# Seven load slots instead of nine for the quads of four feed-forwards, four more scratch blocks, and an earlier read-back of the memory's chunks

## Chip, cores and metric

The kernel runs on one core of one Trainium2 chip. The metric is the device time of one execution, in microseconds (us); less is better. Engines are named as the profile names them: PE does the matrix products (PEld loads its weights), ACT and DVE the elementwise work, POOL little here, and SP mostly issues DMAs.

## What is computed

A two-layer "first block" and then a one-layer "second block" act on 512 tokens of width 1024, in float32. Cut to what matters:

```
def swiglu(h, w_gate, w_up, w_down):
    return (silu(h @ w_gate) * (h @ w_up)) @ w_down          # D_FF = 2816

for l in range(2):                                            # first block
    x = x + 0.5 * swiglu(rmsnorm(x, g_ffn1[l]), ...ffn1[l])
    u = rmsnorm(x, g_mix[l])                                  # mixer: Fourier, dilated and
    ...                                                       # differential attention, gates
    x = x + merged @ w_out[l]
    x = x + 0.5 * swiglu(rmsnorm(x, g_ffn2[l]), ...ffn2[l])
x = rmsnorm(x, g_final)

proj = rmsnorm(x) @ w_in_2                                    # second block ("mixer 2")
attn_o = window_attention(rope(q), rope(k), v, sink)
dn_o   = gated_deltanet(conv(qkv), gate, alpha, beta)         # chunks of 64, 2 directions, 4 heads
x = x + rmsnorm(concat(attn_o, dn_o) @ w_out_2)
x = x + rmsnorm(cross_attention(rmsnorm(x), rmsnorm(mem), w_cq_2, w_ckv_2, w_co_2))
x = x + rmsnorm(swiglu(rmsnorm(x), ...ffn_2))
```

## The kernel before

Every float32 product is done as three products of rounded parts: a weight tile is split into a high part `whi` (by ACT) and the rest `wlo` (by DVE), an activation likewise, and PE adds hi·hi, hi·lo and lo·hi. All weights stream through SBUF once: a 512 KB slab lands in a tile of the pool `raw` (4 KB in each of 128 partitions; five slots), is split into `whi` and `wlo` tiles of 512 columns (pools of five each), and its slot is free again after the last split has read it. Activations and everything else of 512 columns lie in blocks `g` of one pool of NB = 59. Tasks that run beside each other share a count `self.free` of these blocks: `acq(n)` waits until n are free, `rel(n)` gives them back, so NB steers which tasks of a stage may start.

A planner (`drive`) writes the program: tasks are generators with a priority, and the planner's own clock decides which one emits its next instructions. The order on each engine's queue is fixed by the time the kernel is built; on the chip an engine that waits holds everything behind it on its queue. SP's queue issues the weight loads and many small transfers to and from scratch memory in DRAM (`kn_d`, `cs_d`, `nt_d`, `qk_d`, `xinv_d`), in that one order.

**The feed-forwards** (`ffn_task`, four times) begin with a wide start and two pairs of plain slabs (gate and up of columns 256 to 511 and 512 to 767: four raw tiles a pair), and then run eight *quads* n = 0 to 7. A quad takes two feature chunks by a scheme with seven instead of eight products for a two-by-two block product. `fast_load` loads a quad's four weight tiles: two to `raw` (gate, up) and two to the pool `b` (gate, up; four slots); `fast_split(…, 1)` takes a third raw slot for a difference, called q7 here. Nine slots, five raw and four `b`, hold this before. `left(n, i)` puts the splits of product i on the list, `right(n, i)` its matmuls (12 of 256 columns), and `down` puts products of the down projection between them: from quad 2 on, each quad but the last holds two down slabs of 512 KB (four feature chunks each, 24 matmuls of 512 columns); the first six chunks are taken earlier by slabs of 512 KB plus 256 KB (`down(0, 6, …)`). The list runs three items ahead with loads and splits.

**Mixer 2** (`mixer2_task`, from about 2398 us) projects `w_in_2`, runs a convolution, rotary attention in a window and the delta rule (eight chains with triangular inverses through `xinv_d`). Its budget is `self.free = NB - 16 - 9 - 5 - self.mem`. The keys and values of the memory (`memory_proj`, slabs of `w_ckv_2`) run beside it at low priority; that task first reads eight chunks back from DRAM (`mem_d`, on POOL's queue; ten blocks, `self.mem = 10`). `self.rooms` counts the feed-forwards that have reached their last four down slabs. `xinv_d` is set to zero by one DMA of 4128 KB on ACT's queue early in the fourth feed-forward. The list below shows the functions; every instruction of the trace is recorded at line L119, so groups are told apart by tile names.

Of the kernel before, what the change touches and what calls it, by code (L numbers as in the profile page):

```python
# [41 lines left out]
    _o += _w  # L42
MK_COLS = _o
OH_COLS = 1024 + 256 + 64
NB = 59

LK = 4

# [87 lines left out]
class Net:  # L136
    def __init__(self, ctx, tc, ins, dump=None):
        self.ctx, self.tc, self.nc, self.i = ctx, tc, Engines(self, tc.nc), ins
        self.n = 0
        self.dump = dump or {}  # L140
        mk = lambda name, **kw: ctx.enter_context(tc.tile_pool(name=name, **kw))
        self.const = mk("const", bufs=1)
        self.raw = mk("raw", bufs=5)
        self.whi = mk("whi", bufs=5)
        self.wlo = mk("wlo", bufs=5)
        self.pg = mk("pg", bufs=NB)
        self.pt = mk("pt", bufs=2)
        self.psum = mk("psum", bufs=8, space=bass.MemoryType.PSUM)
        self.dram = mk("dram", bufs=1, space=bass.MemoryType.DRAM)

        self.t = 0.0
        self.curp = 9
        self.tasks = []
        self.clk = {"vector": 0.0, "scalar": 0.0, "gpsimd": 0.0}
        self.done = {}
        self.banks = []
        self.ahead = self.gap = False
        self.lock = None
        self.mem, self.kv, self.kvs = 0, [0] * 4, {}
        self.free = NB  # L160
        self.normed = True
        self.rooms = 0
        self.pend = []
# [644 lines left out]
    def ffn_task(self, wg, wu, wd, pre, row, after):  # L808
# [69 lines left out]
        for n in range(nq):  # L878
# [3 lines left out]
                left(n - 1, 4)  # L882
            left(n, 6)
            left(n, 5)
            if n + 1 < nq:
                load(n + 1)
            if n:
                left(n - 1, 3)
            left(n, 7)
            if n == 0:  # L890
                down(0, 6, (4, 6))
            elif n > 1:
                f = 6 + 4 * (n // 2 - 1)
                if n + 1 < nq:
# [737 lines left out]
    def mixer2_task(self, after):  # L1632
        nc, i = self.nc, self.i
        w = i["w_in_2"][0]
        us = self.us
        self.mem = 10
        self.spawn(self.memory_proj(), 7)
        self.free = NB - 16 - 9 - 5 - self.mem
        st = {"cv": {}, "str": False, "k": [False] * 4, "q": [False] * 4, "v": [False] * 4, "nt": [0, 0], "solved": [False] * 2,
              "gate": set(), "win": 0, "B": 0, "dn": 0, "chain": 0}  # L1640
# [641 lines left out]

    def memory_proj(self):
        nc, i = self.nc, self.i
        mp = [(self.g(F32R, [P, 2, 256]), self.g(F32R, [P, 2, 256])) for _ in range(KC // 2)]
        for c in range(KC // 2):
            for k in range(2):
# [267 lines left out]
def build(ctx, tc, ins, out, dump=None, stop=None):  # L2555
# [32 lines left out]
    def between(l):  # L2588
        showx(f"xb{l}")
        if l == 0:  # L2590
            ffn(2, 0, G_FFN1[1], middle)
        else:
            c1.close()
            n.phase(c2, "second")
            ffn(2, 1, G_FINAL, second)
            n.spawn(n.setup_second(), 1)

    def middle():
        showx("xc0")
# [37 lines left out]
```

## Time and profile before

| | us |
|---|---|
| Median of 3 runs | 3406.07 |
| Lowest and highest of them | 3394.13, 3406.7 |
| The profiled execution, its time | 3396.84 |
| Its span | 3395.1 |
| PE busy in it | 3295.8 (97%) |
| DVE busy | 2325.5 (68%) |
| ACT busy | 1562.3 (46%) |

The span is the time between the first and the last instruction of the profiled execution; its time is 1.7 us longer. The stages follow one another: feed-forward 1 to about 375 us, mixer to 850, feed-forwards 2 and 3 to 1190 and 1550, mixer to 2040, feed-forward 4 to 2398, mixer 2 to 2880, cross-attention to 2980, and the last feed-forward. Since PE is busy 97% of the span, the reader looks for the few stretches where it isn't, and for what ended its idle time there.

### The profile page before, as it was taken

What the parts mean: (1) busy time and instruction counts of PE and PEld (TensorE: products, weight loads), DVE (VectorE), ACT (ScalarE), POOL (GpSimd) and SP (SyncE); (2) the same over time, 40 slices, a digit from 0 to 9 for tenths busy, and PEclk for the clock granted to TensorE, in tenths of its full rate; (3) what the DMA queues carried; (4) which work ended last, traced back from release to release, by engine and by line L of the source; (5) the groups of instructions that cost most, each with busy time, mean ns of one, the idle gap of its engine ahead of it and who ended that gap; (6) DMA issues with size and microseconds to landing.
All of it is one profiled execution on the core that took longest, in us unless ns stands there. A gap on an engine that the chain in (4) does not pass through costs nothing.

```text
span 3395.1 us, 50388 instructions
## 1 busy us (share of the span) xinstructions
PE 3295.8 (97%) x19063; PEld 2895.3 (85%) x19063; DVE 2325.5 (68%) x4423; ACT 1562.3 (46%) x3049; POOL 45.2 (1%) x121
## 2 busy tenths in 40 slices
PE   8999999999999999999999999999979888999998
PEld 6899888898889988998888988899868777888887
DVE  6787677656677777776766476777788775764344
ACT  4454545443445454545455444454453344553232
POOL 1000000000000000000000000000000000000000
PEclk9999999999999999999999999999989899999999
DMA  4533433435333333333323368333347522223232
GB/s 134 152 116 94 119 91 93 135 97 181 105 109 110 102 118 100 111 95 118 92 90 118 91 197 159 111 112 94 118 155 203 175 89 91 81 81 100 94 103 70
DMA packets 370948, 391.02 MB, mean 115 GB/s; under 512 B 30801, under 2 KB 325309, under 8 KB 370704
## 3 DMA queue, kind: packets, MB, share of 16 engines
q1 hardware_dynamic: 329248, 332.45, 32.6%
q10 hardware_dynamic: 38464, 47.68, 5.0%
q0 software_dynamic: 2992, 7.67, 0.7%
q8 instruction: 149, 2.44, 0.3%
q14 instruction: 95, 0.78, 0.1%
HBM read 343.56 MB, written 39.98 MB: 113 GB/s over the span
## 4 chain that ended last, share of the span: by engine, by line
PE 89%; DVE 7%; DMA 2%; ACT 1%; issue 1%; SPq 0%; ACTq 0%; DVEq 0%; POOL 0%; POOLq 0%
PE ps L119 89%; DVE g L119 5%; ACT g L119 1%; DVE wlo L119 1%; DMA b<-in_w_ffn_up 0%; DVE sm L119 0%; DMA g<-xinv_d 0%; DMA g<-in_x 0%; DVE b L119 0%; DMA g<-cs_d 0%; ACT whi L119 0%; DVE tmp L119 0%; DMA g<-in_g_ffn 0%; DVE xs L119 0%; SPq L119 0%
## 5 line engine op out<-in xcount | busy, mean ns | idle before, releaser
L119 PE MATMUL ps<-g,whi 128*128 128x512 f32 (+1 forms) x9312 | 2401.4, 348 | 16.0 <-ACT g L119 13.7
L119 PEld LDWEIGHTS ps<-g,whi 128*128 128x128 f32 x9312 | 1620.0, 190 | 234.4 <-ACT g L119 18.4
L119 PE MATMUL ps<-g,wlo 128*128 128x512 f32 (+1 forms) x4656 | 1611.5, 346 | 1.1 <-DVE wlo L119 1.1
L119 ACT ACTIVATE whi<-raw 128x512 fp32r<-128x512 f32 (+1 forms) x1084 | 670.4, 622 | 875.3 <-PE ps L119 776.9
L119 DVE TENSOR_TENSOR wlo<-raw,whi 128x512 fp32r<-128x512 f32 (+1 forms) x1084 | 726.6, 678 | 392.7 <-ACT whi L119 377.7
L119 PEld LDWEIGHTS ps<-g,wlo 128*128 128x128 f32 x4656 | 884.2, 190 | 111.5 <-DVE wlo L119 2.8
L119 DVE TENSOR_TENSOR g<-g,g 128x512 f32<-128x512 f32 (+4 forms) x668 | 401.7, 622 | 74.6 <-ACT g L119 64.8
L119 ACT ACTIVATE g<-g 128x256 fp32r<-128x256 f32 (+4 forms) x560 | 310.7, 571 | 211.8 <-DVE g L119 193.5
L119 DVE TENSOR_TENSOR g<-ps,g 128x512 f32<-128x512 f32 (+3 forms) x350 | 204.2, 598 | 187.5 <-PE ps L119 94.3
L119 PE MATMUL ps<-g,g 128*128 128x128 f32 (+5 forms) x1638 | 264.9, 309 | 14.5 <-DVE g L119 6.3
L119 PE MATMUL ps<-whi,g 128*128 128x256 f32 (+1 forms) x1184 | 255.9, 310 | 0.0
L119 PEld LDWEIGHTS ps<-g,g 128*128 128x128 f32 (+3 forms) x1638 | 223.8, 193 | 35.6 <-DVE g L119 7.2
L119 ACT ACTIVATE whi<-b 128x512 fp32r<-128x512 f32 x192 | 121.2, 632 | 220.5 <-PE ps L119 211.5
L119 DVE SCALAR_TENSOR_TENSOR g<-ps,g 128x512 f32<-128x512 f32 x210 | 149.0, 711 | 98.5 <-PE ps L119 97.8
L119 PEld LDWEIGHTS ps<-whi,g 128*128 128x128 f32 x1184 | 196.6, 192 | 11.3
L119 PE MATMUL ps<-wlo,g 128*128 128x256 f32 (+1 forms) x592 | 183.6, 310 | 3.5 <-DVE wlo L119 3.5
L119 DVE TENSOR_TENSOR wlo<-b,whi 128x512 fp32r<-128x512 f32 x192 | 131.7, 688 | 58.2 <-ACT whi L119 57.9
L119 ACT COPY g<-ps 128x512 f32<-128x512 f32 (+5 forms) x250 | 114.2, 476 | 115.4 <-PE ps L119 103.7
L119 ACT ACTIVATE g<-ps 128x256 fp32r<-128x256 f32 (+6 forms) x239 | 100.3, 433 | 134.2 <-PE ps L119 118.1
L119 DVE TENSOR_TENSOR g<-g,ps 128x512 f32<-128x512 f32 (+1 forms) x171 | 111.4, 655 | 42.1 <-PE ps L119 38.0
L119 PEld LDWEIGHTS ps<-wlo,g 128*128 128x128 f32 x592 | 113.6, 192 | 9.5 <-DVE wlo L119 3.7
L119 ACT ACTIVATE g<-g,sm 128x512 f32<-128x512 f32 (+3 forms) x160 | 89.3, 579 | 37.0 <-DVE sm L119 36.0
(203 smaller groups left out, 1589.8 us busy)
## 6 DMA issues: line engine op xcount, KB each, us to landing
raw<-in_w_ffn_down SPq DMA_DIRECT2D x80, 512.0 KB, 3.4
raw<-in_w_in SPq DMA_DIRECT2D x80, 512.0 KB, 3.9
raw<-in_w_ffn_gate SPq DMA_DIRECT2D x55, 512.0 KB, 3.8
raw<-in_w_ffn_up SPq DMA_DIRECT2D x55, 512.0 KB, 4.0
raw<-in_w_gate SPq DMA_DIRECT2D x48, 512.0 KB, 3.7
raw<-in_w_gate_up SPq DMA_DIRECT2D x44, 512.0 KB, 3.6
b<-in_w_ffn_gate SPq DMA_DIRECT2D x32, 512.0 KB, 3.8
b<-in_w_ffn_up SPq DMA_DIRECT2D x32, 512.0 KB, 3.9
```

The lines of the kernel that those rows point to most:

```text
L119: r = f(*a, **k)
```

## The change

The raw pool has three slots instead of five, which gives 8 KB in each partition; the block pool takes them (63 instead of 59). In a quad the loads of quad n + 1 come on the list after its seventh product instead of after the fifth, and the two early down slabs of chunks 4 to 7 are spread over quads 0 and 1 instead of both standing in quad 0. `memory_proj` is spawned with the fourth feed-forward and waits for `rooms == 4`, so its eight read-backs stand at that feed-forward's end instead of in mixer 2, and `self.mem = 10` is set there.

```diff
-NB = 59
+NB = 63
...
-        self.raw = mk("raw", bufs=5)
+        self.raw = mk("raw", bufs=3)
...
             left(n, 6)
             left(n, 5)
-            if n + 1 < nq:
-                load(n + 1)
             if n:
                 left(n - 1, 3)
             left(n, 7)
-            if n == 0:
-                down(0, 6, (4, 6))
+            if n + 1 < nq:
+                load(n + 1)
+            if n < 2:
+                down(0, 6, (4 + 2 * n,))
...
         us = self.us
-        self.mem = 10
-        self.spawn(self.memory_proj(), 7)
         self.free = NB - 16 - 9 - 5 - self.mem
...
     def memory_proj(self):
         nc, i = self.nc, self.i
+        yield lambda: self.rooms == 4
+        self.mem = 10
...
             ffn(2, 1, G_FINAL, second)
             n.spawn(n.setup_second(), 1)
+            n.spawn(n.memory_proj(), 7)
```

On SP's queue, in a steady quad of the first feed-forward (the numbers behind a tile's name run in the order in which the planner wrote the tiles; `in_w_ffn1_gate` and `_up` are the quad's loads, `_down` the down slabs), it stood so before:

```order
L119 DMA b382_1756<-in_w_ffn1_gate 128x4x256
L119 DMA raw395_1854<-in_w_ffn1_down 128x4x256
L119 DMA raw400_1864<-in_w_ffn1_down 128x4x256
L119 DMA b384_1760<-in_w_ffn1_up 128x4x256
L119 DMA raw438_2095<-in_w_ffn1_gate 128x4x256
L119 DMA raw440_2099<-in_w_ffn1_up 128x4x256
```

and so after:

```order
L119 DMA b448_2164<-in_w_ffn1_gate 128x4x256
L119 DMA raw447_2162<-in_w_ffn1_gate 128x4x256
L119 DMA raw449_2166<-in_w_ffn1_up 128x4x256
L119 DMA b450_2168<-in_w_ffn1_up 128x4x256
L119 DMA raw452_2195<-in_w_ffn1_down 128x4x256
L119 DMA raw461_2244<-in_w_ffn1_down 128x4x256
```

All four loads of the next quad now stand ahead of this quad's two down slabs, and the second down slab was written later (2244 behind 2195, where the two were 10 apart).

On ACT's queue, early in the fourth feed-forward, right behind the zeroing of `xinv_d` (`raw4329` and `raw4330` are the two gate tiles of the slab pair that follows it, `raw4339` and `raw4340` the up tiles, `b43…` tiles of the pool `b` with sums of activations), it stood so before:

```order
L119 ACTIVATE whi4331_21370<-raw4329_21366 128x512
L119 ACTIVATE whi4333_21374<-raw4330_21368 128x512
L119 ACTIVATE g4355_21491<-b4351_21486 128x512
L119 ACTIVATE g4357_21496<-b4353_21488 128x512
L119 ACTIVATE g4359_21501<-b4351_21486 128x512
L119 ACTIVATE whi4335_21378<-raw4329_21366 128x512
L119 ACTIVATE g4361_21506<-b4353_21488 128x512
L119 ACTIVATE whi4337_21382<-raw4330_21368 128x512
```

and so after:

```order
L119 ACTIVATE whi4331_21370<-raw4329_21366 128x512
L119 ACTIVATE g4355_21491<-b4351_21486 128x512
L119 ACTIVATE g4357_21496<-b4353_21488 128x512
L119 ACTIVATE whi4333_21374<-raw4330_21368 128x512
L119 ACTIVATE g4359_21501<-b4351_21486 128x512
L119 ACTIVATE whi4335_21378<-raw4329_21366 128x512
L119 ACTIVATE g4361_21506<-b4353_21488 128x512
L119 ACTIVATE whi4337_21382<-raw4330_21368 128x512
```

Two sums moved ahead of the first split of `raw4330`; that split still stands ahead of the second split of `raw4329`.

On PE, in mixer 2, behind the last `w_in_2` product of the first heads (`ident` rows are transposes; a row with a single `g` spreads per-row factors over a block; `whi51…` with 256 columns are the memory's keys), it stood so before:

```order
L119 MATMUL ps5083_25460<-ident_102,g5031_25193 128x128 x4
L119 MATMUL ps5092_25488<-ident_102,g5032_25205 128x128 x4
L119 MATMUL ps5096_25505<-ident_102,g5054_25328 128x128 x4
L119 MATMUL ps5102_25527<-g5097_25510 128x128 x4
L119 MATMUL ps5106_25545<-ident_102,g5067_25413 128x128 x4
L119 MATMUL ps5108_25552<-g5107_25550 128x128 x4
L119 MATMUL ps5111_25563<-ident_102,g5084_25465 128x128 x4
L119 MATMUL ps5113_25571<-g5112_25568 128x128 x4
L119 MATMUL ps5127_25604<-g5071_25428,whi5118_25587 128x256
```

and so after:

```order
L119 MATMUL ps5095_25521<-ident_102,g5032_25205 128x128 x4
L119 MATMUL ps5099_25534<-ident_102,g5054_25328 128x128 x4
L119 MATMUL ps5102_25543<-g4935_24703,whi5077_25440 128x512
L119 MATMUL ps5102_25543<-g4936_24704,whi5077_25440 128x512
L119 MATMUL ps5102_25543<-g4935_24703,wlo5078_25441 128x512
...
L119 MATMUL ps5104_25560<-g5100_25539 128x128 x4
L119 MATMUL ps5122_25622<-g4935_24703,whi5114_25606 128x512
```

Where eight short groups stood in a row, a `w_in_2` product of 24 matmuls of 512 columns now stands between two of them, and another follows. The slabs of `w_ckv_2` come later in the order than before, behind the other projections.

## Rows read from the trace of the kernel before

**Rows 1.** The page: busy time by engine (part 1), ended chain by engine (part 4).

```profile
PE 3295.8 (97%) x19063; PEld 2895.3 (85%) x19063; DVE 2325.5 (68%) x4423; ACT 1562.3 (46%) x3049; POOL 45.2 (1%) x121
...
PE 89%; DVE 7%; DMA 2%; ACT 1%; issue 1%; SPq 0%; ACTq 0%; DVEq 0%; POOL 0%; POOLq 0%
```

**Rows 2.** Busy times by stretch: length, PE, PEld, DVE, ACT, POOL, clock, DMA.

```profile
850.00:1190.00 340.00, 340.00 (x2102) 307.13 (x2101) 248.66 (x376) 162.93 (x281) 2.19 (x4) 1.00 0.36 105
...
2490.00:2520.00 30.00, 15.69 (x83) 13.68 (x81) 27.74 (x74) 12.30 (x43) 0.00 (x0) 0.73 0.34 113
2520.00:2600.00 80.00, 80.00 (x498) 71.82 (x497) 70.55 (x190) 42.94 (x116) 3.14 (x7) 1.00 0.80 235
2600.00:2660.00 60.00, 56.52 (x348) 49.31 (x347) 44.03 (x81) 20.00 (x40) 0.54 (x1) 0.97 0.61 179
2660.00:2830.00 170.00, 137.68 (x988) 124.23 (x987) 126.11 (x375) 66.41 (x184) 0.00 (x0) 0.92 0.34 104
```

**Rows 3.** PE's waits, 2490 to 2520: total us, times, longest us.

```profile
PE ps L119 <- ACT g L119: 10.8, 3, 7.4
PE ps L119 <- DVE g L119: 3.6, 1, 3.6
```

**Rows 4.** PE's waits, 2660 to 2675.

```profile
PE ps L119 <- DMA g<-qk_d: 4.6, 1, 4.6
PE ps L119 <- DMA g<-xinv_d: 4.6, 2, 3.6
```

**Rows 5.** PE's waits, 170 to 178 (quads 0 and 1 of the first feed-forward).

```profile
PE ps L119 <- ACT g L119: 1.6, 1, 1.6
PE ps L119 <- DVE wlo L119: 0.5, 1, 0.5
```

**Rows 6.** SP's DMA issues in a steady quad: start us, duration us, what.

```profile
1114.59 0.37 SPq L119 DMA_DIRECT2D b<-in_w_ffn_gate  x1
1117.25 3.31 SPq L119 DMA_DIRECT2D raw<-in_w_ffn_down  x2
1123.07 0.37 SPq L119 DMA_DIRECT2D b<-in_w_ffn_up  x1
1129.72 0.37 SPq L119 DMA_DIRECT2D raw<-in_w_ffn_gate  x1
1131.65 0.37 SPq L119 DMA_DIRECT2D raw<-in_w_ffn_up  x1
```

**Rows 7.** DVE, the same quad, in order of time.

```profile
1125.41 0.69 DVE L119 TENSOR_TENSOR wlo<-raw,whi 128x512 fp32r<-128x512 f32 x1
1126.13 1.23 DVE L119 TENSOR_TENSOR raw<-raw,raw 128x1024 f32<-128x1024 f32 x1
```

**Rows 8.** PE, the same quad; the 128x512 rows are a down product.

```profile
1131.62 0.63 PE L119 MATMUL ps<-g,whi 128*128 128x512 f32 x2
...
1137.09 0.62 PE L119 MATMUL ps<-g,whi 128*128 128x512 f32 x2
```

**Rows 9.** DMA issues of the whole run: xcount, KB each, median us to landing.

```profile
raw<-in_w_ffn_down SPq DMA_DIRECT2D x80, 512.0 KB, 3.4
...
xinv_d<-g ACTq DMA_DIRECT2D x1, 4128.0 KB, 42.4
raw<-in_w_ffn_down SPq DMA_DIRECT2D x16, 256.0 KB, 2.6
```

**Rows 10.** Landing times of all down loads (in_w_ffn_down), us min/median/max.

```profile
DMA to landing us min/median/max: 2.6/3.4/8.7
```

**Rows 11.** DMA queues and issues, 2083 to 2126 (q10 is ACT's queue, q1 SP's).

```profile
q10 hardware_dynamic: 8208, 4.23, 79.0%
q1 hardware_dynamic: 3589, 3.56, 35.9%
...
raw<-in_w_ffn_up SPq DMA_DIRECT2D x3, 512.0 KB, 14.3
```

**Rows 12.** Landings of the two raw loads issued between 2094.4 and 2096.3.

```profile
DMA to landing us min/median/max: 16.5/17.7/18.9
```

**Rows 13.** Landing of the raw load issued at 2114.9.

```profile
DMA to landing us min/median/max: 9.8/9.8/9.8
```

**Rows 14.** PE there; the four raw tiles of two slabs are first used here.

```profile
2105.92 0.62 PE L119 MATMUL ps<-g,whi 128*128 128x512 f32 x2
...
2108.64 0.62 PE L119 MATMUL ps<-g,whi 128*128 128x512 f32 x2
...
2111.36 0.62 PE L119 MATMUL ps<-g,whi 128*128 128x512 f32 x2
...
2114.08 0.62 PE L119 MATMUL ps<-g,whi 128*128 128x512 f32 x2
```

**Rows 15.** ACT at the start of the fourth feed-forward.

```profile
2104.59 0.63 ACT L119 ACTIVATE whi<-raw 128x512 fp32r<-128x512 f32 x1 [2.91 <-PE ps L119]
...
2105.65 1.14 ACT L119 ACTIVATE whi<-raw 128x512 fp32r<-128x512 f32 x2
...
2111.06 0.63 ACT L119 ACTIVATE whi<-raw 128x512 fp32r<-128x512 f32 x1 [3.75 <-DMA raw<-in_w_ffn_up]
...
2114.25 0.61 ACT L119 ACTIVATE whi<-raw 128x512 fp32r<-128x512 f32 x1
```

## The prediction

> **What bounds the kernel now.** I read the page first, then the busy times by stretch, then PE's waits in the stretches where PE is not full, then SP's issues and the landing times. The page says that PE is busy 3295.8 of 3395.1 us and that PE's own work is 89% of the chain that ended last [rows 1]. In a feed-forward stretch there is nothing to win: PE is busy 340.00 of 340 us [rows 2]. What there is lies in mixer 2. There PE idles 30 - 15.69 = 14.3 us from 2490 to 2520, nothing from 2520 to 2600, 3.5 us from 2600 to 2660 and 170 - 137.68 = 32.3 us from 2660 to 2830 [rows 2], 50.1 us in all. The first idle stretch waits for results of ACT and DVE, 10.8 and 3.6 us [rows 3], and DVE is busy 27.74 of those 30 us [rows 2]: a chain of small vector work (convolution, norms) with only transposes between on PE. The last one begins with waits for transfers of the delta rule, 4.6 us for `qk_d` and 4.6 for `xinv_d` [rows 4]. TensorE's granted clock is 1.00 of full speed where PE is full and 0.73 and 0.92 in the two idle stretches [rows 2].
>
> So the change takes slots from stages that are full and gives blocks to the one stage that isn't. The working below asks what fewer slots cost there and what four blocks are worth here.
>
> **Steady quads (n = 2 to 7), three raw slots.** Call S the start of a quad's first down product, 1131.62 in the trace; its 24 matmuls end 5.47 us later, at 1137.09, where the second begins [rows 8]. Before, the two down slabs are issued at about 1117.2 and 1120.2 (two issues that take 3.31 us together [rows 6]), 11 us and more ahead of S. After, the three slots are held by gate, up and q7, and the first down slab gets q7's slot of the quad when its last split ends: 1125.41 + 0.69 = 1126.10, that is S - 5.5 [rows 7]. It lands a median 3.4 us later [rows 9], at S - 2.1; ACT's split takes 0.63 [rows 15] and DVE's 0.69 [rows 7], so it is ready at S - 0.8. The second down slab needs the first one's slot, free when both halves are split, about S; it lands at S + 3.4, is ready at S + 4.75, and is wanted at S + 5.47. Margins of 0.8 and 0.7 us, on a path that had 10: at the median nothing, but the slowest landing of the run was 8.7 us [rows 10] and would cost 4 to 5. There are 24 such pairs. I take **+2 us** (a slow landing every tenth slab at half a microsecond); bounds 0 and 15 (0.6 us for each pair). The next quad's gate and up loads, issued at 1129.72 and 1131.65 before and ahead of the down slabs now [rows 6], gain time. What is queued behind the waiting down slab on SP is the next quad's loads, whose slots come free later anyway.
>
> **Quads 0 and 1.** Each now has one slab pair of 512 and 256 KB. The second waits for the first one's slot, issued about S, lands in 2.6 us [rows 9], and has its high part at S + 3.3, its low part at S + 4.0. PE wants them after 12 matmuls of 5.47/24 us, at S + 2.7 and S + 3.2. Short by 0.8 to 0.9 us, eight times: **+7 us**; bounds 0 (the first slab's early halves done sooner) and 16. In the first feed-forward PE waits 1.6 and 0.5 us at this place now [rows 5], behind quad loads that stood behind the down slabs on SP; they now stand ahead: **-2 us**, at best that, at worst 0.
>
> **The start of the fourth feed-forward.** Under the zeroing of `xinv_d` (42.4 us [rows 9], 79.0% of the engines' time from 2083 to 2126 [rows 11]) raw loads land very late: two issued at 2094.5 and 2095.8 after 16.5 and 18.9 us [rows 12], one issued at 2114.9 after 9.8 [rows 13]. Before, four tiles of the next two slabs had landed or were on their way ahead of it, and PE started them at 2105.92, 2108.64, 2111.36 and 2114.08 [rows 14] without a stall, though ACT already waited 3.75 us for one of these transfers [rows 15]. With three slots each load is issued two tiles later. The second tile (2108.64) takes the issue of 2094.5 and lands about 2111.0: 3 us late. The third takes that of 2095.8 and lands at 2114.7: another 1. The fourth needs the slot of `raw4329`, whose second split stands on ACT behind the first split of the late second tile; it is issued near 2114.9, and by the row of that time lands at 2124.7, is split at 2125.3, and is wanted at 2114.08: 11 us in all, the earlier delays included. By the undisturbed 3.7 us it would be 2118.6, 5 us in all. I take the row of the same instant: **+11 us**, bounds 5 and 15.
>
> The Trainium skill says in "DMA: Bandwidth & Descriptors", section "Queues, rings and completion order", that each of the 16 DMA engines goes round the queues that have work, a packet from each. By that a load beside one other queue would get about half the engines, 3.4 us would become 7, and this term would be 0, as an estimate from that page; the 16.5 and 18.9 us of the trace speak against it, and the sum goes by the trace.
>
> **Mixers 1 and the last two stages.** PE is full in the mixers, the SP order of their slabs is the same, and no transfer of a raw tile stands among PE's waits there, so I take three slots to be enough: **0**, bounds -1 and +4. The read-back of the memory's chunks moves eight POOL transfers of 256 KB into the end of the fourth feed-forward, where POOL has no other work and SP's down slabs share the DMA engines: 0, bounds 0 and 3.
>
> **Mixer 2.** With four more blocks the planner puts `w_in_2` products between the transposes where PE stood idle, and the memory's slabs later. Total PE and DVE work is unchanged. From 2490 to 2600 DVE is busy 27.74 + 70.55 = 98.3 of 110 us [rows 2], so the stretch can't shrink by more than 11.7; from 2600 to 2660 the 3.5 us can go. In the last stretch DVE is busy 126.11 of 170 us, so PE's 32.3 us are the bound. All four head pairs now come to the deltas together, which gives more chains beside each other, but less projection work is left to put between. I take 11.7 + 3.5 + a third of 32.3 (10), **-25 us**. Bounds: -50 (every idle stretch), and +15 for the case below.
>
> **The rivals.** (a) *The delta stretch is filled too*: four pairs of chains beside each other cover each other's transfers and PE's clock stays up. For it: the waits there are latency, not work. It gives 50 instead of 25: 3396.84 + 18 - 50 = 3365. (b) *The slots bind in the quads*, the slower side. Place: the two down slabs of a quad, with 0.7 us of margin each. If transfers land 1 us later than the median, because all of a quad's loads now stand together ahead of them on SP, each of 24 pairs costs 1 to 1.3 us, and the early quads 1 us more: 30 + 15 + 11 - 2 - 25 gives 3396.84 + 29 = 3426. It decides from a landing of 4.2 us; the median of 3.4 speaks against it. The Trainium skill's rule in "DMA: Bandwidth & Descriptors", section "Rules for kernel authors", to issue a DMA early and wait for it late, is on this rival's side; the trace has no quad with so late an issue. (c) *The fill is only moved*: products taken for 2490 to 2520 are missing after 2660, the delta chains last as long as before and PE idles 14 us more there. Then mixer 2 gives 0 and the sum is 3396.84 + 18 = 3415. It decides if the stretch of the deltas doesn't get shorter than its 170 us. (d) *The change doesn't do what it says*, the blocks go unused: the order on PE speaks against it, since the products already stand elsewhere.
>
> **How the numbers follow.** The sum is +2 +7 -2 +11 +0 -25 = -7 us against the profiled execution, 3396.84: 3390. That execution lies 9.2 us under the median of the runs shown, 3406.07; against the median it is 3399. The runs lie in two groups some 12 us apart, and I can't tell in which the median after falls, so I predict the middle, **3394 us**. Its own range, with the terms' bounds, is 3375 to 3415. Chances: this forecast 0.46, (a) 0.22, (b) 0.13, (c) 0.16, (d) 0.03. The range for 8 in 10 reaches from (a) to the near part of (b): 3364 to 3422. A measurement of this kernel can tell about 0.5%, 17 us, from no change. Faster than 3389 are all of (a) and a third of the forecast, 0.38; slower than 3423 are most of (b) and a third of (c), 0.17; within, 0.45.
>
> **What would show it.** Right: PE stays full in the steady quads, with short waits for `wlo` or `whi` twice in each feed-forward's quads 0 and 1; one wait of some 11 us in two or three pieces near 2105 to 2125, behind raw loads under the zeroing; PE almost full from 2490 to 2520, and the deltas' end some 10 to 15 us nearer to the start of mixer 2 than before even after that. Wrong: waits for raw loads in every quad (b); the idle time reappearing in the delta stretch, with no shorter mixer 2 (c); a delta stretch with PE above 95% and the clock at 1.00 (a). The largest guess is the third of the 32.3 us; the next is the landing under the zeroing.

## The result: 20 us slower, where a few microseconds less were forecast

The changed kernel takes 3419.41 us (median of 5 runs, 3417.32 to 3424.64), the kernel before 3399.27 us (median of 5, 3394.13 to 3406.7). The ratio is 1.0058, with a 95% interval of 1.0039 to 1.0076. The forecast was 3394 us; the time lies inside the range (3364 to 3422) but on the other side of no change. The spans of the two profiled executions are 3395.1 and 3415.5 us, so the traces hold the same 20 us.

The page of the changed kernel, busy times and ended chain, answers to [rows 1]:

```profile
PE 3306.1 (97%) x19063; PEld 2895.5 (85%) x19063; DVE 2309.7 (68%) x4423; ACT 1549.3 (45%) x3049; POOL 45.0 (1%) x121
...
PE 84%; DVE 5%; DMA 4%; ACT 2%; issue 1%; ACTq 0%; DVEq 0%; SPq 0%
```

PE has ten microseconds more of busy time (3306.1 against 3295.8) and DMA has come into the chain, 4% where it was 2%. That the number of PE instructions is the same (x19063) says that no work was added.

To see where the time went, I marked in both traces the moment at which PE starts the first product with each stage's weights, and took differences of stage lengths. Before the change these marks lie at 385.2, 883.7, 1232.3, 1583.8, 2082.3 and 2431.0 us (mixer, feed-forwards 2 and 3, mixer, feed-forward 4, mixer 2), which is 10 to 42 us behind the round times that the description of the kernel gives. A positive number is time lost against the profiled execution of the kernel before:

| Stage | changed kernel, us | forecast, us |
|---|---|---|
| Feed-forward 1 | +11.8 | +0.25 (a quarter of 2 + 7, and -2) |
| Mixer, layer 1 | +2.8 | 0 |
| Feed-forward 2 | +4.2 | +2.25 |
| Feed-forward 3 | +2.0 | +2.25 |
| Mixer, layer 2 | +3.3 | 0 |
| Feed-forward 4 | +14.9 | +13.25 (11 of them at its start) |
| Mixer 2 and all behind it | -18.4 | -25 |
| Sum | +20.5 | -7 |

How exact is such a number? Three kernels below have the first feed-forward word for word as before, and it came out 2.1 to 3.1 us longer in them; the unchanged feed-forwards and mixers behind it agree within 1 us. Stages in which PE waits repeat less well. Seven kernels, the changed one among them, have the same order on PE in feed-forward 2, and it lost 4.2 to 7.7 us in them; five share the changed kernel's mixer 2, which came out 16.8 to 22.8 us shorter. So the rows of stages with waits are good to about 3 us, and mixer 2's to about 6.

The busy times of the changed kernel from 850 to 1190 us (the end of the mixer and most of feed-forward 2) and for three stretches of mixer 2 (columns as in [rows 2]; the stretches are counted from mixer 2's start, which is 39 us later than before):

```profile
850.00:1190.00 340.00, 338.09 (x2020) 299.97 (x2019) 237.12 (x368) 155.25 (x272) 2.18 (x4) 1.00 0.37 110
2469.90:2559.90 90.00, 76.71 (x351) 60.13 (x350) 71.98 (x171) 38.61 (x94) 4.28 (x8) 0.92 0.41 130
2559.90:2699.90 140.00, 120.95 (x700) 106.07 (x699) 111.60 (x261) 62.11 (x155) 3.15 (x7) 0.94 0.71 203
2699.90:2851.40 151.50, 141.32 (x1110) 130.99 (x1109) 127.28 (x374) 67.69 (x191) 0.54 (x1) 0.98 0.43 135
```

The first 90 us and the next 140 us of mixer 2 in the kernel before:

```profile
2431.00:2521.00 90.00, 70.35 (x335) 55.92 (x334) 71.81 (x170) 40.09 (x100) 4.26 (x8) 0.87 0.38 127
2521.00:2661.00 140.00, 136.52 (x846) 121.10 (x845) 115.33 (x270) 63.26 (x156) 3.68 (x8) 0.99 0.72 212
```

From 850 to 1190 us PE is no longer full, 338.09 of 340 us. In mixer 2 the stretch of the deltas is now 151.5 us long where it had been 170, with a granted clock of 0.98 (0.92 before). The first 90 us hold 76.71 us of PE work instead of 70.35. The 140 us between them hold less than before, 120.95 instead of 136.52: part of the idle time has moved there.

### The profile page after: what moved, and what is told of

Same layout as the page of the kernel before. It is cut to its first block, busy times and chain, and to the rows that moved or that the text cites. A ratio compares the mean times of both kernels' runs of the same rounds, so it can differ in the third digit from the quotient of the medians.

```text
span 3415.5 us, 50278 instructions
## 1 busy us (share of the span) xinstructions
PE 3306.1 (97%) x19063; PEld 2895.5 (85%) x19063; DVE 2309.7 (68%) x4423; ACT 1549.3 (45%) x3049; POOL 45.0 (1%) x121
## 4 chain that ended last, share of the span: by engine, by line
PE 84%; DVE 5%; DMA 4%; ACT 2%; issue 1%; ACTq 0%; DVEq 0%; SPq 0%
PE ps L119 84%; DVE g L119 3%; DMA raw<-in_w_ffn_down 2%; DVE wlo L119 1%; ACT whi L119 1%; ACT g L119 1%; DVE sm L119 0%; DMA raw<-in_w_ckv 0%; DMA raw<-in_w_ffn_gate 0%; DMA raw<-in_w_ffn_up 0%; DMA g<-in_tab 0%; DMA g<-cs_d 0%; DVE tmp L119 0%; ACTq L119 0%; DMA g<-gd 0%
## 5 line engine op out<-in xcount | busy, mean ns | idle before, releaser
L119 PEld LDWEIGHTS ps<-g,whi 128*128 128x128 f32 x9312 | 1627.0, 191 | 263.2 <-ACT whi L119 25.3
L119 ACT ACTIVATE whi<-raw 128x512 fp32r<-128x512 f32 (+1 forms) x1084 | 655.8, 620 | 933.8 <-PE ps L119 623.9
L119 DVE TENSOR_TENSOR wlo<-raw,whi 128x512 fp32r<-128x512 f32 (+1 forms) x1084 | 716.3, 677 | 433.8 <-ACT whi L119 420.2
L119 PE MATMUL ps<-g,g 128*128 128x128 f32 (+5 forms) x1638 | 256.2, 304 | 9.5 <-ACT g L119 6.4
L119 PEld LDWEIGHTS ps<-g,g 128*128 128x128 f32 (+3 forms) x1638 | 216.4, 188 | 29.6 <-ACT g L119 7.8
```

The costliest lines, as they stand in the source:

```text
L119: r = f(*a, **k)
```

## What ends the idle time now

**Feed-forward 1.** PE's waits between 100 and 200 us, columns as in [rows 3], first in the changed kernel, then in the kernel before:

```profile
PE ps L119 <- ACT g L119: 6.8, 1, 6.8
PE ps L119 <- ACT whi L119: 5.3, 3, 2.9
PE ps L119 <- DVE wlo L119: 0.8, 2, 0.6
...
PE ps L119 <- ACT g L119: 1.7, 2, 1.6
PE ps L119 <- DVE wlo L119: 0.5, 1, 0.5
```

12.9 us, where it was 2.2. The chain of waits shows one of them, at a down slab; the list of DMA issues from 120 to 131 us names what else is loaded then:

```profile
122.24 7.60 DMA raw<-in_w_ffn_down
...
129.93 0.64 ACT whi L119
...
130.61 1.46 PE ps L119 x4
...
bt<-bias_d ACTq DMA_DIRECT2D x2, 448.0 KB, 6.5
```

This slab, of 512 KB, needs 7.6 us to land, against the median of 3.4 [rows 9], and two tables of the mixer (`bt`) are loaded beside it on ACT's queue. That they delay it isn't tested by a run. The largest wait, 6.8 us, ends with ACT itself. ACT at that place, in order of time (the number in brackets is the idle time before the instruction and what ended it; the ACTq rows are DMA issues, which don't count as busy):

```profile
154.88 1.85 ACTq L119 DMA_DIRECT2D g<-bias_d  x4
...
157.31 0.63 ACT L119 ACTIVATE whi<-b 128x512 fp32r<-128x512 f32 x1 [5.23 <-DMA g<-bias_d]
...
161.77 0.33 ACTq L119 DMA_DIRECT2D db_d<-g  x1
162.97 0.63 ACT L119 ACTIVATE g<-g 128x512 f32<-128x512 f32 x1 [3.99 <-DVE g L119]
...
163.97 0.39 ACTq L119 DMA_DIRECT2D db_d<-g  x1
...
164.94 1.87 ACTq L119 DMA_DIRECT2D g<-bias_d  x4
166.85 0.59 ACT L119 COPY g<-ps 128x512 f32<-128x512 f32 x1 [3.25 <-DMA db_d<-g]
```

ACT is idle 5.23, 3.99 and 3.25 us, for two reasons. The setup builds its tables with DMAs on ACT's own queue, and the write of a finished table (`db_d`) waits for a DVE sum of two loaded pieces; so before the issue at 161.77 nothing moves on ACT. And the issues themselves take 0.33 to 0.52 us each, 11.6 us for the 30 table transfers from 143.8 to 177.3 us: the last idle time, 3.25 us, is almost all issuing, though the profile names a transfer as what ended it. Every split of a weight behind an issue on ACT waits too. The kernel before has the same 30 issues there, and idle times of ACT of 3.23 and 3.17 us that end the same way, with only 2.2 us of waits on PE; that more was already split ahead then is my reading.

The 11.8 us are a net number. Up to 100 us the changed kernel is ahead (PE busy 87.03 us, before 81.45). Then come the 10.7 us of additional waits, and behind them a lower clock: the granted clock from 130 to 170 us is 0.82, before it was 1.00.

```profile
130.00:170.00 40.00, 31.14 (x191) 28.20 (x192) 24.91 (x39) 13.90 (x24) 0.95 (x3) 0.82 0.51 150
...
130.00:170.00 40.00, 39.84 (x263) 36.13 (x262) 27.56 (x43) 14.40 (x26) 0.95 (x3) 1.00 0.63 187
```

**Feed-forward 2**, where no tables are in the way (900 to 1240 us):

```profile
PE ps L119 <- ACT g L119: 1.2, 3, 0.5
PE ps L119 <- ACT whi L119: 0.7, 2, 0.3
```

Five short waits, 1.9 us together. The kernel before has none in this stretch.

**Feed-forward 4.** PE's waits at its start and its busy time there, then ACT's queue and the zeroing in the list of DMA issues, then the landing of the two raw loads issued at 2118.5 and 2119.8:

```profile
PE ps L119 <- ACT whi L119: 7.1, 2, 5.6
PE ps L119 <- DVE wlo L119: 1.2, 1, 1.2
...
2130.00:2150.00 20.00, 11.68 (x43) 8.25 (x42) 10.07 (x17) 7.67 (x14) 0.00 (x0) 0.90 0.94 169
```

```profile
q10 hardware_dynamic: 8208, 4.23, 83.6%
...
xinv_d<-g ACTq DMA_DIRECT2D x1, 4128.0 KB, 38.5
```

```profile
DMA to landing us min/median/max: 15.0/15.8/16.7
```

This is the wait of the forecast, and its size nearly too: the loads land after 15.0 and 16.7 us, PE waits 8.3 us behind them in three pieces, the granted clock falls to 0.90, and the stage is 12.0 us late when its first down slab starts.

**The mixers of the first block.** A new wait of 2.8 us in each, here the one of the first, where the kernel before waits 0.7 us:

```profile
PE ps L119 <- DVE sm L119: 2.8, 1, 2.8
```

**Mixer 2.** POOL's read-backs of the memory's chunks, first before, then in the changed kernel:

```profile
2430.55 3.39 POOL L119 DMA_DIRECT2D g<-mem_d  x6 [393.31 <-PE ps L119]
```

```profile
2536.71 0.54 POOL L119 DMA_DIRECT2D g<-mem_d  x1 [476.64 <-DMA raw<-in_w_in]
...
2552.78 1.06 POOL L119 DMA_DIRECT2D g<-mem_d  x2 [5.88 <-DVE g L119]
```

They are not at the end of the fourth feed-forward (mixer 2's first product comes at 2469.9 in this trace) but 67 us into mixer 2. They stand later in the program than before, not earlier, so this part of the change does not do what its description says.

## Experiments

All ratios are against the kernel before, timed beside each; the stage lengths are taken from the profiled executions as above, in us against the kernel before. That one profiled execution (3396.84 us) lies some 6 us below the medians of the kernel before beside the experiments (3402.26 to 3404.26 us), so a row adds up to a few microseconds more than its median says. In three rows the profiled execution itself is off its median: e2 3.6 us below, e5 3.4 and e7 9.3 us above.

| Kernel | slots, blocks, budget of mixer 2 | FF 1 | mixer | FF 2 | FF 3 | mixer | FF 4 | mixer 2 and on | median |
|---|---|---|---|---|---|---|---|---|---|
| changed kernel | 3, 63, 33 | 11.8 | 2.8 | 4.2 | 2.0 | 3.3 | 14.9 | -18.4 | 3419.4 |
| e1, quads only | 3, 59, 19 | 15.2 | 0.1 | 5.8 | 4.5 | 0.4 | 17.3 | 2.1 | 3442.2 |
| e2, early read-back only | 5, 59, 29 | 2.1 | 0.1 | 0.0 | -0.6 | 0.3 | 0.0 | -31.8 | 3370.5 |
| e3, read-back as before | 3, 63, 23 | 13.9 | 2.7 | 7.7 | 3.0 | 4.7 | 18.1 | -24.1 | 3423.8 |
| e4, zeroing in 2 KB rows | 3, 63, 33 | 14.1 | 1.3 | 7.1 | 4.2 | 3.1 | 3.1 | -22.5 | 3407.7 |
| e5, e4 with budget 29 | 3, 63, 29 | 13.3 | 2.8 | 5.5 | 5.2 | 4.8 | 5.0 | -25.5 | 3404.5 |
| e6, tables late | 3, 63, 33 | 1.0 | 7.2 | 5.2 | 3.4 | 5.7 | 17.5 | -22.7 | 3413.4 |
| e7, all three mended | 3, 63, 33 | 4.2 | 2.5 | 6.0 | 4.1 | 0.2 | 5.1 | -16.8 | 3393.0 |
| e8, e2 with the 2 KB zeroing | 5, 59, 29 | 3.1 | 0.5 | 0.1 | -0.9 | 0.1 | 0.0 | -29.1 | 3371.8 |
| e9, new order, five slots | 5, 59, 29 | 13.8 | 0.0 | 0.2 | -0.7 | 0.3 | 0.1 | -27.2 | 3384.9 |
| e10, old order, three slots | 3, 59, 29 | 16.1 | 0.2 | 4.3 | 4.4 | 0.7 | 22.0 | -28.8 | 3415.3 |
| e11, budget 33 | 5, 59, 33 | 3.1 | 0.3 | 0.0 | -0.8 | 0.3 | -0.1 | -25.6 | 3374.2 |
| e12, four slots, old order | 4, 61, 31 | -3.8 | 0.1 | 2.0 | -0.8 | 0.3 | 6.2 | -14.8 | 3385.2 |
| e13, mixers' budget as before | 3, 63, 33 | 15.1 | 0.3 | 6.2 | 3.4 | 0.2 | 16.6 | -22.8 | 3417.2 |
| e14, e2 with later tables | 5, 59, 29 | 6.8 | 0.0 | 0.0 | -0.7 | 0.2 | 0.0 | -25.3 | 3377.9 |

**e1: the quads alone.**

```diff
-        self.raw = mk("raw", bufs=5)
+        self.raw = mk("raw", bufs=3)
...
(the new order of loads and down slabs in ffn_task; 59 blocks and memory_proj as before)
```

> The kernel before with three raw slots and the new order in the quads alone: 59 blocks, the memory read back in mixer 2 as before. Theory 1 (the slots cost in the feed-forwards, the blocks moved the mixers): the four feed-forwards lose 11.8 + 4.2 + 2.0 + 14.9 = 33 us as between the two traces, the mixers nothing, mixer 2 nothing: 3399 + 33 = 3432 us, and the waits of 2.8 us for small DVE results near 694 and 1902 are gone. Theory 2 (three slots cost in the mixers too): another 6 us there, 3438 us, with those waits still in place.

Measured: 3442.2 us, ratio 1.0113 (1.0098 to 1.0128). The feed-forwards lose 43 us, the mixers 0.1 and 0.4, mixer 2 gains nothing. Theory 1 holds in kind: the quads' edit costs the feed-forwards and not the mixers. By the medians it costs 39 us; the 43 us instead of 33 are 3 to 4 us more in the first feed-forward and about 2 us in each other, little more than these terms' spread.

**e2: the early read-back alone.**

```diff
-        self.mem = 10
-        self.spawn(self.memory_proj(), 7)
         self.free = NB - 16 - 9 - 5 - self.mem
...
     def memory_proj(self):
         nc, i = self.nc, self.i
+        yield lambda: self.rooms == 4
+        self.mem = 10
...
             n.spawn(n.setup_second(), 1)
+            n.spawn(n.memory_proj(), 7)
```

> The kernel before with the memory's chunks read back at the end of the fourth feed-forward, five slots and 59 blocks. Theory 1 (the four blocks are what shortens mixer 2): no difference, 3399 us within 4. Rival (the earlier read-back shortens mixer 2): 18 us less, 3381 us, with mixer 2 ending 18 us sooner after its start.

Measured: 3370.47 us, ratio 0.9906 (0.989 to 0.9923): 33 us *faster* than before, and the lowest median here. Theory 1 fails: without one additional block this edit shortens mixer 2 by 31.8 us, more than the whole change does. Its busy times from mixer 2's start:

```profile
2432.90:2522.90 90.00, 77.91 (x362) 61.27 (x361) 73.02 (x173) 40.65 (x99) 2.54 (x5) 0.94 0.38 121
2522.90:2662.90 140.00, 125.90 (x790) 113.21 (x790) 120.69 (x276) 65.23 (x156) 5.42 (x12) 0.95 0.72 210
2662.90:2800.00 137.10, 127.99 (x1006) 117.94 (x1005) 114.01 (x354) 63.46 (x184) 0.00 (x0) 0.99 0.46 146
```

The delta stretch is 137 us long instead of 170, at a clock of 0.99.

Why, if the reads don't come earlier? The answer is in the code. While the feed-forward's main task holds the planner's lock for its slabs, no task of priority 4 and up may run. `memory_proj` has priority 7, so when `rooms` becomes 4 it can't run until the feed-forward is done, and then `mixer2_task`, of priority 5, goes first. It computes `self.free = NB - 16 - 9 - 5 - self.mem` while `self.mem` is still 0; the ten blocks of the read-back are never subtracted. Mixer 2's budget becomes 29 in e2 where it had been 19, and 33 in the changed kernel. Three more variants, built but not timed, show it in their order. The kernel before with the read-back in its old place and a budget of 29 written in has the same instructions in the same order as e2, on all engines; e2 with 10 subtracted by hand has those of the kernel before; the changed kernel with the read-back in its old place and 33 written in has its own. So the edit *is* the budget, nothing else. With the larger budget the value heads of the delta rule are no longer held back (their first product comes 63 us into mixer 2, before 119), the planner emits the `w_in_2` products at once, and the memory's slabs (first product at 172 us, before 86), which came into the gap, are left as filling for the delta stretch.

**e3: the changed kernel with the read-back in mixer 2.**

```diff
+        self.mem = 10
+        self.spawn(self.memory_proj(), 7)
         self.free = NB - 16 - 9 - 5 - self.mem
...
-        yield lambda: self.rooms == 4
-        self.mem = 10
...
-            n.spawn(n.memory_proj(), 7)
```

> The changed kernel with the memory's chunks read back in mixer 2 as before. Theory 1 (the blocks shorten mixer 2): the same as the changed kernel, 3419 us within 4. Rival (the earlier read-back does): mixer 2 gets its 18 us back, 3437 us.

Measured: 3423.83 us, ratio 1.0059 (1.0044 to 1.0074). As theory 1 said, the time hardly changes: mixer 2 is 24.1 us shorter, with a budget of 23. So each of the two edits alone gives mixer 2 most of what there is (24 and 32 us), and both together no more (17 to 23). Both raise one number: from 19 to 23, to 29, to 33. For the 23 no run separates the number from the four blocks themselves.

**e4: the zeroing in rows of 2 KB.**

```diff
-        nc.scalar.dma_start(self.xinv.rearrange("k c t p q -> (k c t p q)").rearrange("(p n q) -> p n q", p=P, q=P + 1),
-                            z[:, 0:P + 1].unsqueeze(1).to_broadcast([P, 64, P + 1]))
+        flat = self.xinv.rearrange("k c t p q -> (k c t p q)").rearrange("(p m) -> p m", p=P)
+        nc.scalar.dma_start(flat[:, 0:8192].rearrange("p (n q) -> p n q", q=S), z.unsqueeze(1).to_broadcast([P, 16, S]))
+        nc.scalar.dma_start(flat[:, 8192:8256], z[:, 0:64])
```

> The changed kernel with the zeroing of xinv_d in rows of 2 KB instead of 516 bytes, the same bytes and the same place. Theory 1 (the raw loads under the zeroing cost the 12 us at the start of the fourth feed-forward): the zeroing ends in some 15 to 20 us instead of 42, the raw loads there land within 8 us, the wait falls from 8.3 us to under 2, and the time is 3407 to 3411 us. Rival (the wait there is the three slots' own, whatever the zeroing does): no difference, 3419 us.

Measured: 3407.68 us, ratio 1.0011 (1.0002 to 1.0021), 12 us under the changed kernel, as theory 1 expected. ACT's queue and the issue (columns as in [rows 11]), then the busy times where the changed kernel waited 8.3 us:

```profile
q10 hardware_dynamic: 2208, 4.23, 23.6%
...
xinv_d<-g ACTq DMA_DIRECT2D x1, 4096.0 KB, 13.5
```

```profile
2136.00:2156.00 20.00, 20.00 (x90) 16.57 (x89) 17.52 (x29) 11.81 (x20) 0.00 (x0) 1.00 0.36 106
...
DMA to landing us min/median/max: 3.8/4.4/5.0
```

The same 4 MB are 2208 packets instead of 8208 and take 13.5 us instead of 38.5. The two raw loads that had landed after 15.0 and 16.7 us are issued at 2124.2 and 2125.5 us here, 1 to 2 us before the zeroing ends, land within 5.0 us (the last row), and PE is full.

**e5: budget 29.** The kernel of e4 with one line more:

```diff
-        self.free = NB - 16 - 9 - 5 - self.mem
+        self.free = 29
```

> The changed kernel with the 2 KB zeroing and with mixer 2's budget set to 29 blocks instead of the 33 it gets. Theory 3 (what shortens mixer 2 is the budget, which the move raised by ten because the subtraction now comes too late; 29 is enough and the four blocks add nothing): mixer 2 is shortened by 32 us as in the kernel with the early read-back alone, 3398 us. Rival (three slots cost mixer 2 some 10 us whatever the budget): no difference from 3408 us.

Measured: 3404.51 us, ratio 1.0006 (0.9996 to 1.0015). Mixer 2 is 25.5 us shorter than before, against 22.5 in e4 and 31.8 in e2. The time is 3 us below e4's, not 10, and the two intervals overlap, so no difference between 33 and 29 is shown here. Nor is one to e2 in mixer 2: with one and the same order on PE it came out 31.8, 29.1, 27.2 and 25.3 us shorter in e2, e8, e9 and e14. What can be said is that four more blocks on top of a raised budget bring nothing that these runs can see.

**e6: the tables late.**

```diff
-        yield 10.0
+        yield lambda: self.rooms == 1
         self.setup_dilated()
```

> The changed kernel with the setup's bias and Fourier tables (some 30 small transfers on ACT's queue at 121 to 177 us) issued at the end of the first feed-forward instead of in its quads 0 and 1. Theory 1 (down slabs land late beside these transfers, and ACT's queue stands still behind them): the first feed-forward loses 3 us instead of 12, the other stages as in the changed kernel, 3410 us. Rival (the quads 0 and 1 lose this much with three slots anyway): first feed-forward still 10 us or more late, 3419 us.

Measured: 3413.44 us, ratio 1.0031 (1.0021 to 1.004). PE's waits between 100 and 200 us, and those in the mixer behind it (380 to 860):

```profile
PE ps L119 <- ACT whi L119: 5.0, 3, 2.6
PE ps L119 <- DVE wlo L119: 0.5, 1, 0.5
```

```profile
PE ps L119 <- DVE sm L119: 2.8, 1, 2.8
PE ps L119 <- DVE wlo L119: 1.8, 1, 1.8
```

Feed-forward 1 loses 1.0 us instead of 11.8. The longest wait, the one behind ACT's table issues, is gone, and with it most of the lower clock (0.96 from 130 to 170 us). So the tables on ACT's queue do most of it. The other half of theory 1 doesn't come out: the waits for `whi` are 5.0 us where they were 5.3, and the down slab lands as late as in the changed kernel, with the two `bt` loads of 121 us, which this edit doesn't move, still beside it:

```profile
122.88 7.38 DMA raw<-in_w_ffn_down
```

These 5.5 us of waits are offset by the gain before 100 us, which e6 has too. And the mixer, which needs the tables and whose order on PE changes with them, now loses 7.2 us instead of 2.8: part of the gain is given back. With the mixers' old budget it loses 2.5 us with the late tables (e7) and 0.3 without (e13).

**e7: all three mended.** The changed kernel with e4's and e6's edits and, in `mixer_task`:

```diff
-        self.free = NB - 22
+        self.free = 37
```

> The changed kernel with the late tables, the 2 KB zeroing and the mixers' budget of 37 blocks as before. Theory 1 with all three causes: 12 us less at the fourth feed-forward's start, 9 in the first, 6 in the two mixers: 3392 us. If the mixers' 6 us are three slots' cost and not the other order: 3398 us.

Measured: 3393.01 us, ratio 0.9976 (0.9966 to 0.9985): the expected 3392. The profiled execution, 3402.28 us, is the longest of the ten, and its stages hold 9 us that the median doesn't have; which stage has them isn't known. In it feed-forward 1 loses 4.2, the mixers 2.5 and 0.2, feed-forward 4 5.1; feed-forwards 2 and 3 still lose 6.0 and 4.1 (three slots in the quads), and mixer 2 is 16.8 us shorter. By the medians three slots, mended so, come out 22 us behind e2, which changes nothing in the feed-forwards.

**e8: early read-back and the 2 KB zeroing.** The edits of e2 and e4 on the kernel before.

> The kernel before (five slots, 59 blocks) with the early read-back and the 2 KB zeroing. Theory 1: five slots cover the zeroing already, so no difference to the early read-back alone, 3370 us within 4. Rival (the long zeroing also costs five slots something): 3365 us or less.

Measured: 3371.75 us, ratio 0.9909 (0.9892 to 0.9925): no difference to e2. Five slots cover the long zeroing; a price of it shows only with fewer.

**e9: the new order with five slots.** The changed kernel with

```diff
-NB = 63
+NB = 59
...
-        self.raw = mk("raw", bufs=3)
+        self.raw = mk("raw", bufs=5)
```

> The changed kernel's order of loads and down slabs in the quads, with five slots and 59 blocks (mixer 2's budget is 29). Theory 4 (it is the number of slots, not the order, that costs the feed-forwards 33 to 43 us): the four feed-forwards lose no more than 2 us together against the kernel before, and with mixer 2's 30 us the time is 3370 us. Rival (the order costs, for it puts a quad's loads ahead of its down slabs): 3385 us or more.

Measured: 3384.93 us, ratio 0.9944 (0.993 to 0.9959). The rival's number, and half of theory 4 falls. Feed-forwards 2 to 4 lose nothing (0.2, -0.7, 0.1): there the slots cost, not the order. But feed-forward 1 loses 13.8 us by the order alone, where the unchanged one lost 2.1 to 3.1. ACT in its quads 0 and 1, in order of time:

```profile
162.38 2.84 ACTq L119 DMA_DIRECT2D g<-bias_d  x5
165.33 0.63 ACT L119 ACTIVATE whi<-raw 128x512 fp32r<-128x512 f32 x1 [3.29 <-DMA g<-bias_d]
...
173.16 0.63 ACT L119 ACTIVATE whi<-raw 128x512 fp32r<-128x512 f32 x1 [2.05 <-DMA g<-in_tab]
...
176.22 1.83 ACTq L119 DMA_DIRECT2D g<-bias_d  x4
178.09 0.59 ACT L119 COPY g<-ps 128x512 f32<-128x512 f32 x1 [3.77 <-DMA g<-bias_d]
```

Again ACT issues table transfers or waits for their data, with splits of weights behind. My reading is that the first feed-forward's quads stand beside the tables only as long as enough is split ahead, and that either edit, the order or the slots (e10), uses that up.

**e10: the old order with three slots.** The edits of e2, and

```diff
-        self.raw = mk("raw", bufs=5)
+        self.raw = mk("raw", bufs=3)
```

> The kernel before's order in the quads with three slots, 59 blocks and mixer 2's budget of 29. Theory 4: three slots cost at least what they cost in the new order, and more in the steady quads, where the down slabs stand behind the next quad's raw loads on SP, which now wait for slots: every steady quad 2 us or more, feed-forwards together 43 + 50 us or more, 3460 us. Rival (the old order copes as well): 43 us, 3413 us.

Measured: 3415.28 us, ratio 1.0033 (1.0018 to 1.0047), the rival's number. I had expected steady quads 2 us slower each; feed-forwards 2 and 3 lose 4.3 and 4.4 us, the same as in the new order. The new order therefore buys nothing there that these runs can see. In the first feed-forward three slots alone cost 16.1 us; PE's waits from 100 to 375 us:

```profile
PE ps L119 <- ACT whi L119: 9.1, 5, 3.4
PE ps L119 <- ACT g L119: 6.5, 4, 4.1
```

In the fourth the price is larger than in the new order, 22.0 us for the whole stage. Why the steady quads cope so well with the old order I didn't follow further.

**e11: budget 33 with five slots.** The kernel before with

```diff
-        self.free = NB - 16 - 9 - 5 - self.mem
+        self.free = 33
```

> The kernel before, five slots and 59 blocks, with mixer 2's budget set to 33 (19 before, 29 with the early read-back). If the budget alone matters and more is better: 3366 us or less. If 29 is past the knee, as 29 against 33 in the changed kernel suggests (3 us better at 29): 3370 to 3376 us. If it asks for more blocks than the pool has at once, waits on blocks appear in mixer 2: over 3380 us.

Measured: 3374.19 us, ratio 0.9912 (0.9897 to 0.9927). Mixer 2 is 25.6 us shorter, inside the 25.3 to 31.8 us of the kernels with 29, and the interval overlaps with e2's: whether 29 is better than 33 isn't shown. The 33 blocks are promised from a pool that has no more than before, and the gain is there all the same: it comes from the count and not from additional blocks.

**e12: four slots and 61 blocks**, old order, early read-back.

> Four slots and 61 blocks with the order of the quads of the kernel before, early read-back (mixer 2's budget is 31). Theory 4, with one slot fewer than five: most of the cost of three slots is gone, the start of the fourth feed-forward loses 3 us or less, the feed-forwards together under 10 us, mixer 2 gains 28: 3380 us. Rival (a steady quad needs the fifth slot, as q7 and two down slabs beside gate and up): 3395 us or more.

Measured: 3385.23 us, ratio 0.9943 (0.9929 to 0.9958), between the two expectations. The feed-forwards together lose 3.6 us, so one slot less is nearly free there; at the start of the fourth one wait is left:

```profile
PE ps L119 <- ACT whi L119: 2.5, 1, 2.5
```

But mixer 2 has only 14.8 us of gain with a budget of 31, where 29 and 33 gave 25 to 32 with five slots. Since e10, with three slots, has 28.8, the slots are an unlikely cause; that the planner's order isn't a smooth function of the budget is my guess, from one trace.

**e13: the mixers' budget as before.** The changed kernel with `self.free = 37` in `mixer_task`.

> The changed kernel with the two mixers' budget of blocks left at 37 as before (NB - 22 gave 41). Theory 5 (the larger budget lets the planner put the mixers in another order, and that order costs the 2.8 and 3.3 us): the mixers lose 0.3 us or less each, as with three slots and 59 blocks, and the time is 3413 us. Rival (the blocks' other places in the pool do it): still 2 to 3 us each, 3419 us.

Measured: 3417.21 us, ratio 1.0044 (1.0029 to 1.0059). The mixers lose 0.3 and 0.2 us instead of 2.8 and 3.3, as theory 5 says, and PE's waits in the first mixer are those of the kernel before:

```profile
PE ps L119 <- ACT g L119: 0.7, 1, 0.7
```

The time is only 2 us better, not the expected 6, and no difference that the intervals show: the first feed-forward and feed-forward 2 came out 3 and 2 us longer in this run, which is the spread of these terms. So the cause is shown by the waits and the stage lengths, not by the time.

**e14: early read-back and later tables.** The edits of e2, and

```diff
-        yield 10.0
+        yield 40.0
         self.setup_dilated()
```

> The kernel before with the early read-back, and the setup's bias tables asked for 30 us later in the first feed-forward. Theory (the tables' transfers hold up ACT where quads 0 and 1 have little split ahead): PE's waits of 2.1 us near 171 to 176 go, 3368 us. Rival (five slots and the old order cover nearly all of it): no difference to 3370 us within 4.

Measured: 3377.86 us, ratio 0.9925 (0.9908 to 0.9941). Neither expectation: feed-forward 1 loses 6.8 us instead of 2.1. Thirty microseconds later is no better place for these transfers; the rest of the difference to e2 is mixer 2, with the same order on PE and inside its spread.

## Why the forecast was wrong, step by step

**The steady quads and quads 0 and 1** (+2 and +7): right in kind, and small. Feed-forwards 2 and 3 lose 4.2 and 2.0 us in the changed kernel, and 2.0 to 7.7 in the kernels with the same quads, where 2.25 each were forecast: the size was some 2 us too low for each. The waits are a few short ones, as described. Three slots and not the order do this (e9 against e10). By the forecast's own times the early quads' shortfall is 0.6 and 0.8 us, not 0.8 to 0.9, which is 1 to 2 us less in the sum.

**The first feed-forward** (a share of these, and -2): this step failed, and by the most. I counted slots against a median landing and looked at what SP's queue holds. What decides there is ACT's queue, on which thirty table transfers are issued, some of them waiting for their own data, in front of the splits; the slab that landed after 7.6 us adds to it. The row that should have warned me was in front of me: of the 2.1 us of [rows 5] 1.6 ended with ACT, and I read them as a late load. The stage lost 11.8 us where 0.25 was forecast; e6 takes the tables away and 1.0 is left, as the net of 5.5 us of waits and a faster start that the forecast didn't have.

**The start of the fourth feed-forward** (+11): right. 12.0 us, by the mechanism described, with landings of 15.0 and 16.7 us; e4 removes it. The round-robin rule of the Trainium skill ("DMA: Bandwidth & Descriptors", "Queues, rings and completion order"), which by my estimate gave 0 here, would have misled: beside the zeroing in 516-byte rows a load took over four times its median of 3.4 us, not twice.

**The mixers** (0, bounds -1 and +4 for both and the last stages): this step failed. I took the order of their slabs on SP as unchanged, and it isn't: a slab of `w_in` moved ahead of six slabs of `w_gate`. Their budget is NB - 22, so it rose from 37 to 41, and the order changed with it: 6.1 us, of which 0.5 are left in e13.

**Mixer 2** (-25): the sign is right, -18.4, and the mechanism is half right. The first idle stretch was filled in part and the delta stretch became shorter, 151.5 us instead of 170; that the 140 us between them would hold 15.6 us less PE work wasn't foreseen. But I credited four blocks, from 19 to 23. The budget went to 33, since the subtraction comes too late. This also settles rival (d): I had given it 0.03 because the products had moved in the order on PE. The edit indeed didn't do what it says, the reads came 106 us later in the span (67 us later in mixer 2's own time) instead of earlier, and POOL's rows in the order would have shown it; the products had moved because of the larger budget.

**The rivals.** (b) had the right sign and nearly the number (3426), but not the mechanism: the steady quads' pairs of down slabs cost little; the first feed-forward's tables, the zeroing and the mixers' order make up 30 of the 39 us that are lost before mixer 2. (c)'s number, 3415, is the nearest of all, by luck: what it describes didn't happen, since the stretch of the deltas got shorter. (a) is what e2 nearly does: 32 of its 50 us, with PE busy 93% of the delta stretch at a clock of 0.99. That the time lies inside the stated range is luck too: the losses ahead of mixer 2 came to 39 us, where 18 were forecast.

In the forecast's terms the trace reads 21 (the feed-forwards' quads) + 12 (the zeroing) + 6 (the mixers) - 18 = 21 us, where the forecast had 7 + 11 + 0 - 25 = -7. Of the 27.5 us between the two, the first feed-forward has 11.6, the two mixers 6.1 and mixer 2 6.6, which is no more than mixer 2's spread.

## What to carry to other kernels

A count that steers a planner, like a budget of blocks, is a parameter of the whole order: when an edit changes it, every stage that is planned with it must be read anew, and the order of the moved instructions says whether the edit did what it claims. Ahead-of-time slots are not worth the same everywhere: price them where other traffic, or another queue's work, delays what they hold, and not only by the median landing in the quiet stretches. And when two edits come together, try each alone; here one of them, alone, is 33 us faster than before (3370.47 us, ratio 0.9906) and the other 39 us slower. A stage length from one trace has a spread of its own: compare it in kernels that have the same instructions there before reading a few microseconds.

## What the runs showed of the hardware that I had not expected

Zeroing 4 MB of DRAM took 38.5 to 42.4 us in rows of 516 bytes and 13.5 us in rows of 2 KB, from the same queue; in two traces, raw loads of 512 KB issued beside the first kind landed after 15.0 to 18.9 us where 3.4 is the median of the down slabs. A sequence of DMA issues on ACT's queue, 0.33 to 0.52 us each and some of them waiting for their own inputs, kept ACT from its splits for 3 to 5 us at a time.
